# mLSTM denominators: GpSimd adds three heads' weighted scores over the source blocks, TensorE sums each direction over the partitions once

## The chip, the core and the metric

The kernel runs on one core of a Trainium2 chip. The metric is the device time of one execution in microseconds (us). The engines are named as in the profile: PE is TensorE's matmul, PEld its weight load, DVE is VectorE, ACT is ScalarE, POOL is GpSimd, SP issues the DMAs. SBUF is the working memory of 128 partitions; PSUM holds the results of matmuls.

## The reference, cut to what matters

Two layers of a transformer block on 256 latent and 256 context tokens of width 1024. Each layer has an mLSTM branch of four heads of width 128, two attentions, a merge and a feed-forward part. The first layer computes latent and context tokens, the second latent tokens only. For one head, one direction and one chunk of tokens the mLSTM is

```python
s = jnp.einsum('bhtd,bhsd->bhts', qc, kc) * w          # scores times decay weights
num = a[..., None] * jnp.einsum('bhtd,bhde->bhte', qc, C) + jnp.einsum('bhts,bhse->bhte', s, vc)
den = a * jnp.einsum('bhtd,bhd->bht', qc, n) + jnp.sum(s, axis=-1)
hc = num / jnp.maximum(jnp.abs(den), jnp.exp(-m_t))[..., None]
```

Both directions (forward and reversed) are computed and added. What the change concerns is `den`: for every head, direction and target token, the sum of the weighted scores over all source tokens.

## The kernel before, in words

The kernel doesn't scan chunk by chunk. It takes all 512 tokens (columns 0 to 255 latent, 256 to 511 context) as four source blocks `sb` of 128 tokens, 0 and 1 latent, 2 and 3 context. For a head `h` and a direction `d` it forms a tile per source block: the 128 source tokens on the partitions, the targets as columns. In the first layer the number of target columns `n` is 512, in the second 256. The columns that a block can reach differ (`lo` to `hi` in `mlstm_weights`): in the first layer 512, 512, 256 and 128 columns forwards, 512, 384, 256 and 128 backwards.

The stages of a head are these.

- `mlstm_weights` (L572): `rep` (L566) spreads a row of running maxima over the partitions by a matmul into a PSUM tile of the tag `tr`; ACT takes the exponential into a tile of tag `q` (forwards) or `wk` (backwards) at L586; POOL zeroes the future by an affine select (L592 forwards, L596 backwards), on all four blocks in the first layer and on blocks 0 and 1 in the second.
- `mlstm_scores` (L601) takes the source blocks in two halves, (2, 3) and then (0, 1). Per block one PE matmul of keys and queries goes into a PSUM tile of tag `s`, of which there are two; DVE multiplies it into the weights of both directions, in place (L608). The `s` tiles of the second half can be written only when DVE has read those of the first.
- `mlstm_values` (L611): per weighted tile a PE matmul with the values adds to the numerator, in `acc` forwards and in `tr` backwards. Then, for the same tiles, a PE matmul with a stationary operand of 32 columns of `cst` sums the tile over its partitions into the tile `den` (tag `mm`). Which of the four groups of 32 PSUM partitions it writes depends on the block's parity and the direction: `c = 32 * (2 * (sb % 2) + d)`. Row `4 * d + h` within the group is the head's; the other 31 rows get zeros.
- `mlstm_heads` (L627) runs the scores one half ahead of the values, head after head; `other(g)` adds the query projections of the windowed attention behind heads 2 and 3.
- `mlstm_den` (L649) copies `den`, adds the four groups by one matmul and takes the reciprocal.

All matmuls are issued at L135 and are known by their tiles: `tr<-pt,sel` is `rep`, `s<-m,m` a score, `acc<-q,y` and `tr<-wk,y` the numerators, `mm<-q,cst` and `mm<-wk,cst` the denominators, `mm<-hx,whi` and `mm<-hx,wlo` a projection. An f32 matmul shows as two instructions in the trace.

The order of the instructions on each engine is set when the program is built, by a scheduler that takes what it holds ready; an engine works strictly in that order. All DMAs go through SP. Weight blocks arrive in `wraw` and are split by ACT (L192) and DVE (L193) into a high and a low part, some blocks ahead of their use.

Of the kernel before, what the change touches and what calls it, by code (L numbers as in the profile page):

```python
# [11 lines left out]
F32R = mybir.dt.float32r  # L12
AF = mybir.ActivationFunctionType
ALU = mybir.AluOpType
# [6 lines left out]
RS_K = 0.5 * RS_C  # L21
# [16 lines left out]

# feature blocks of the input projection, in the order in which they are packed
B_Q, B_K, B_V, B_O = 0, 4, 8, 12  # L40
# [3 lines left out]
NW_IN = 52  # L44
# the gates have a bias row only: their weights come apart
B_IF = NW_IN
NB_IN = NW_IN + 1

# columns of the packed shape constants
C_ID, C_ONE, C_BD, C_MOD, C_COS, C_SIN = 0, 128, 129, 131, 133, 389  # L50
C_MA, C_MB, C_SUM, C_STRIP, C_IFS = 645, 773, 901, 965, 1028
NCST = 1156

# columns of the packed small parameters
P_BIN = 0
# [24 lines left out]
class Blank:  # L80
    """Stands for the chip while the order of the weight blocks is collected."""

# [10 lines left out]
class Net:  # L93
    def __init__(self, nc, tc, es, io, out, plan=None):
# [7 lines left out]
            "hx": pool("hx", 16), "m": pool("m", 9), "y": pool("y", 16), "wk": pool("wk", 5), "pt": pool("pt", 4),  # L102
            "q": pool("q", 12), "n": pool("n", 3), "g": pool("g", 2), "h": pool("h", 6),
            "sm": pool("sm", 12), "sn": pool("sn", 6), "sc": pool("sc", 8),
# [36 lines left out]

# [1 line left out]
    def split_weights(self, hi, lo, raw, src):  # L143
# [3 lines left out]
    def weights(self, name, idx, kb=8, width=128):  # L147
        """High and low parts of a block in pieces of width columns, fetched in the order in which they are used."""
        key = (name, idx, kb, width)
        self.used.append(key)  # L150
        if self.plan is None:
            return [(self.nc, self.nc)] * (kb * 128 // width)
        while self.sent < min(len(self.plan), len(self.used) + self.ahead):
            k = self.plan[self.sent]
            self.ready[k] = self.fetch(*k)
            self.sent += 1
        return self.ready.pop(key)
# [30 lines left out]

# [1 line left out]
    def split(self, hi, lo, x):  # L190
# [4 lines left out]
    def rms_columns(self, parts, n, inv, cols, nc_):  # L195
        """1 / sqrt(mean + EPS) of every token, up to the factor RS_K that the gains carry, tokens on the partitions.

        parts: squares, features on the partitions; cols: [128, nc_] picks the features of each group."""
        nc = self.nc
# [21 lines left out]
    def inv_rms(self, parts, n, inv, cols, nc_, tag):  # L221
        """The same on all the partitions, tokens along the free axis."""
        nt = n // 128
# [8 lines left out]

# [1 line left out]
    def setup(self):  # L234
# [54 lines left out]
    def mod_dve(self, blk):  # L289
        """One block of the modulation: features on the partitions, sums along the free axis."""  # L290
        nc = self.nc
# [47 lines left out]

# [1 line left out]
    def sumsq(self, parts, j, c0, c1, on_dve=False):  # L341
# [33 lines left out]

# [1 line left out]
    def bias(self, l, blk):  # L377
# [22 lines left out]
    def proj_v(self, l, hx):  # L400
        """Values of all the heads of the mLSTM, tokens on the partitions."""
        pss = [self.big(t) for t in ("mm", "s", "mm", "s")]
# [14 lines left out]
    def proj_values(self, l, hx):  # L417
        """Values of both attentions, tokens on the partitions: by two blocks of tokens, then by attention."""
        pss = [self.big("mm") for _ in range(2)]
# [75 lines left out]

# [1 line left out]
    def gate_weights(self, l):  # L497
# [4 lines left out]
    def gate_part(self, ps, w, k, x):  # L502
        """One feature block of the 16 gate columns; four blocks side by side on the array."""
        r = 32 * (k % 4)
        self.mm(ps[r:r + 32], w[:, 32 * k:32 * k + 32], x, k < 4, k >= 4)
# [54 lines left out]
    def stack_rows(self, rows, n):  # L560
        """Rows as F32R high parts on partitions 0-63 and low parts on 64-127."""
        o = self.big("pt", F32R)
# [9 lines left out]
    def mlstm_weights(self, h, n, rows):  # L572
        """Decay weights by (direction, source block): the tile and the columns that hold them."""
        nc = self.nc
# [36 lines left out]
    def mlstm_values(self, h, n, half, v, wt, num, den):  # L611
        parts = []
        for d in range(2):
            for i, sb in enumerate(MSB[half][::1 - 2 * d]):
# [4 lines left out]
                for a, b in pieces:  # L619
                    self.mm(num[d][:, a:b], v[sb][:, 128 * h:128 * h + 128], w[:, a:b], i + half == 0, i + half == 2)  # L620
                    parts.append((d, sb, w, a, b))
        for d, sb, w, a, b in parts:
            r, c = 4 * d + h, 32 * (2 * (sb % 2) + d)
            self.mm(den[c:c + 32, a:b], self.cst[:, C_STRIP + 31 - r:C_STRIP + 63 - r], w[:, a:b],
                    False, h == NH - 1 and half == 1)

    def mlstm_heads(self, n, q, k, v, rows, den, other):  # L627
        """Numerators of all the heads; the scores run one half of the source blocks ahead of the values."""
        nums, prev = [], None
        for h in range(NH + 1):  # L630
            for half in range(2):
                if h < NH:
                    if half == 0:
                        wt = self.mlstm_weights(h, n, rows)
                    self.mlstm_scores(n, half, q[h], k[h], wt)
                if prev is not None:
                    g, ghalf, gwt = prev
                    if ghalf == 0:
                        num = [self.big("acc"), self.big("tr")]
                    self.mlstm_values(g, n, ghalf, v, gwt, num, den)  # L640
                    if ghalf == 1:
# [20 lines left out]
    def mlstm_sum(self, h, n, nums, r, sums):  # L662
        """Both directions of a head together, and the sums of its squares as rows: high and low parts of a
        row lie 16 partitions apart."""
        nc = self.nc
# [36 lines left out]

# [1 line left out]
    def scores(self, l, pair, q, k, ctx, window, qb):  # L704
# [59 lines left out]
    def attention(self, l, heads, n, ys, fill):  # L764
        """heads: (pair, q, k, v, window) by name of the result; one unit of scores runs ahead of the values."""
        nc = self.nc
# [30 lines left out]

# [1 line left out]
    def gate(self, l, i, j, hx, n):  # L799
# [16 lines left out]

# [1 line left out]
    def residual(self, l, which, j, ps, c0, c1):  # L818
# [45 lines left out]
    def scaled_hx(self, hx, l, j):  # L864
        """The block before the norm's factor, and the shift as the columns after it."""
        nc = self.nc
# [55 lines left out]

# [1 line left out]
    def layer(self, l, hx, n, first, gates):  # L924
# [322 lines left out]
def build(arrays):  # L1247
    nc = bacc.Bacc("TRN2", target_bir_lowering=False, num_devices=1)
    io = {k: nc.dram_tensor(k, a.shape, F32, kind="ExternalInput").ap() for k, a in arrays.items()}
# [14 lines left out]
```

## Time and profile before

| what | value |
|---|---|
| median of 3 runs | 1526.93 us (1526.5 to 1527.32) |
| profiled execution, span | 1523.1 us |
| PE busy | 1507.0 us, 99% |
| DVE busy | 1067.4 us, 70% |
| ACT busy | 748.9 us, 49% |
| POOL busy | 31.1 us, 2% |
| chain that ended last | PE 98% |

The span is the profiled execution's time from its first instruction to its last. The trace has no wall time of its own for that execution; the median of the runs is 3.8 us above the span, and this is taken as what lies around it. The denominators stand in two short stretches: about 136 to 178 us (first layer) and 1048 to 1078 us (second layer).

### The profile page before, as it was taken

What the parts mean: (1) busy time and instruction counts of PE and PEld (TensorE: products, weight loads), DVE (VectorE), ACT (ScalarE), POOL (GpSimd) and SP (SyncE); (2) the same over time, 40 slices, a digit from 0 to 9 for tenths busy, and PEclk for the clock granted to TensorE, in tenths of its full rate; (3) what the DMA queues carried; (4) which work ended last, traced back from release to release, by engine and by line L of the source; (5) the groups of instructions that cost most, each with busy time, mean ns of one, the idle gap of its engine ahead of it and who ended that gap; (6) DMA issues with size and microseconds to landing.
All of it is one profiled execution on the core that took longest, in us unless ns stands there. A gap on an engine that the chain in (4) does not pass through costs nothing.

```text
span 1523.1 us, 25242 instructions
## 1 busy us (share of the span) xinstructions
PE 1507.0 (99%) x8999; PEld 1241.7 (82%) x9000; DVE 1067.4 (70%) x2664; ACT 748.9 (49%) x1525; POOL 31.1 (2%) x72
## 2 busy tenths in 40 slices
PE   8999999999999999999999999999999999999997
PEld 4586677777777889888888888887788889999997
DVE  5396397666558846889588677654788766776765
ACT  4444455555574334532233233653556665665553
POOL 0001100000000000000000000000100000000000
PEclk9999999999999999999999999999999999999999
DMA  9472012112125632466455553341133335566662
GB/s 333 164 237 76 24 50 91 56 62 63 63 83 180 187 97 78 151 215 209 151 193 185 189 173 118 95 131 57 59 112 111 98 105 160 168 192 182 182 179 91
DMA packets 112591, 203.74 MB, mean 134 GB/s; under 512 B 12496, under 2 KB 16336, under 8 KB 112464
## 3 DMA queue, kind: packets, MB, share of 16 engines
q1 hardware_dynamic: 112464, 202.11, 42.0%
q8 instruction: 71, 1.16, 0.3%
q14 instruction: 56, 0.46, 0.1%
HBM read 201.02 MB, written 1.05 MB: 133 GB/s over the span
## 4 chain that ended last, share of the span: by engine, by line
PE 98%; DVE 1%; ACT 0%; issue 0%; DMA 0%; ACTq 0%; DVEq 0%
PE mm L135 65%; PE s L135 21%; PE acc L135 5%; PE tr L135 4%; PE tr L748 3%; DMA h<-w_if 0%; DVE h L1059 0%; ACT m L372 0%; DVE wlo L193 0%; ACT hx L192 0%; ACT whi L192 0%; DVE y L669 0%; DVE q L485 0%; ACT h L274 0%; PE tr L555 0%
## 5 line engine op out<-in xcount | busy, mean ns | idle before, releaser
L192 ACT ACTIVATE whi<-wraw 128x512 fp32r<-128x512 f32 (+1 forms) x558 | 345.7, 625 | 515.3 <-PE mm L135 352.9
L135 PE MATMUL mm<-hx,whi 128*128 128x512 f32 (+2 forms) x2128 | 548.6, 344 | 1.9 <-ACT hx L192 1.6
L193 DVE TENSOR_TENSOR wlo<-wraw,whi 128x512 fp32r<-128x512 f32 (+1 forms) x558 | 374.4, 681 | 171.8 <-ACT whi L192 159.8
L135 PEld LDWEIGHTS mm<-hx,whi 128*128 128x128 f32 x2128 | 364.6, 189 | 60.8 <-issue 15.0
L135 PE MATMUL mm<-hx,wlo 128*128 128x512 f32 (+2 forms) x1064 | 362.3, 341 | 0.1
L135 PE MATMUL mm<-y,whi 128*128 128x256 f32 (+1 forms) x1024 | 259.7, 332 | 0.0
L135 PEld LDWEIGHTS mm<-hx,wlo 128*128 128x128 f32 x1064 | 201.1, 189 | 26.5 <-issue 4.4
L135 PE MATMUL s<-hx,whi 128*128 128x512 f32 (+2 forms) x800 | 193.5, 331 | 0.0
L135 PEld LDWEIGHTS mm<-y,whi 128*128 128x128 f32 x1024 | 176.6, 190 | 18.5 <-issue 1.5
L135 PE MATMUL mm<-y,wlo 128*128 128x256 f32 (+1 forms) x576 | 188.6, 328 | 0.0
L135 PEld LDWEIGHTS s<-hx,whi 128*128 128x128 f32 x800 | 135.6, 189 | 16.2 <-issue 2.9
L135 PE MATMUL s<-hx,wlo 128*128 128x512 f32 (+2 forms) x400 | 132.6, 332 | 0.5 <-DVE wlo L193 0.5
L135 PEld LDWEIGHTS mm<-y,wlo 128*128 128x128 f32 x576 | 109.5, 190 | 10.0 <-issue 0.5
L298 DVE SCALAR_TENSOR_TENSOR q<-q,q 128x512 f32<-128x512 f32 x160 | 105.4, 689 | 0.1
L298 DVE SCALAR_TENSOR_TENSOR h<-q,q 128x512 bf16<-128x512 f32 x160 | 104.7, 688 | 0.1
L135 PE MATMUL mm<-m,whi 128*128 128x256 f32 (+1 forms) x320 | 85.2, 320 | 0.0
L135 PEld LDWEIGHTS s<-hx,wlo 128*128 128x128 f32 x400 | 75.6, 189 | 10.2 <-issue 2.5
L135 PE MATMUL s<-q,q 128*128 128x512 f32 (+1 forms) x192 | 80.0, 424 | 0.0
L750 ACT ACTIVATE pt<-tr 128x512 f32<-128x512 f32 (+1 forms) x96 | 46.7, 525 | 29.6 <-PE tr L748 29.0
L135 PEld LDWEIGHTS mm<-m,whi 128*128 128x128 f32 x320 | 56.9, 190 | 4.4
L823 DVE SCALAR_TENSOR_TENSOR X<-mm,m,X 128x256 f32<-128x256 f32 x88 | 40.2, 482 | 24.8 <-PE mm L135 24.6
L135 PEld LDWEIGHTS s<-q,q 128*128 128x128 f32 x192 | 36.1, 188 | 24.8 <-issue 21.0
(233 smaller groups left out, 1771.8 us busy)
## 6 DMA issues: line engine op xcount, KB each, us to landing
wraw<-w_ff SPq DMA_DIRECT2D x256, 256.0 KB, 3.0
wraw<-w_in SPq DMA_DIRECT2D x206, 256.0 KB, 2.7
q<-w_mod SPq DMA_DIRECT2D x160, 256.0 KB, 3.0
wraw<-w_br SPq DMA_DIRECT2D x48, 256.0 KB, 2.7
y<-w_mod SPq DMA_DIRECT2D x32, 256.0 KB, 5.4
wraw<-w_o SPq DMA_DIRECT2D x32, 256.0 KB, 2.7
X<-x SPq DMA_DIRECT2D x4, 512.0 KB, 5.3
q<-cc SPq DMA_DIRECT2D x8, 256.0 KB, 4.7
```

What stands on the lines that cost most here:

```text
L135: self.nc.tensor.matmul(out, a, b, start=start, stop=stop)
L192: nc.scalar.activation(out=hi, in_=x, func=AF.Copy)
L193: return nc.vector.tensor_tensor(out=lo, in0=x, in1=hi.bitcast(F32), op=ALU.subtract)
L298: nc.vector.scalar_tensor_tensor(out=junk if v == 0 else raw, in0=raw, scalar=1.0, in1=self.cb[v][c], op0=ALU.mult, op1=ALU.mult, accum_ou ...
L748: self.nc.tensor.transpose(pt[:, 128 * b:128 * b + 128], p[:, 128 * b:128 * b + 128], self.ident)
L750: self.nc.scalar.activation(out=pts[-1][:, :nk], in_=pt[:, :nk], func=AF.Copy)
L823: nc.vector.scalar_tensor_tensor(out=self.X[:, j, a:b], in0=ps[:, a - c0:b - c0], scalar=self.mod[l][which][:, j, v:v + 1], in1=self.X[:, ...
```

## The change

Three of the four heads no longer have a denominator matmul per tile. When both halves of such a head are scored, POOL adds the tiles of a direction over the source blocks into one tile `pv` of 1024 columns (both directions side by side), and PE sums each direction over the partitions once: six matmuls, issued together between the two halves of the last head's values. The last head keeps its matmuls. The new matmuls of head `i` use the group of 32 rows that `i % 2` and the direction give. A pool `pv` of three tiles is added, and to make room the scratch for dynamic DMAs is set to 1024 bytes. All else in the diff is comments and blank lines.

```diff
+            "q": pool("q", 12), "pv": pool("pv", 3), ...
...
                     self.mm(num[d][:, a:b], v[sb][:, 128 * h:128 * h + 128], w[:, a:b], i + half == 0, i + half == 2)
                     parts.append((d, sb, w, a, b))
+        if h < NH - 1:
+            return
         for d, sb, w, a, b in parts:
-            r, c = 4 * d + h, 32 * (2 * (sb % 2) + d)
-            self.mm(den[c:c + 32, a:b], self.cst[:, C_STRIP + 31 - r:C_STRIP + 63 - r], w[:, a:b],
-                    False, h == NH - 1 and half == 1)
+            self.mlstm_den_part(den, h, d, sb % 2, w, a, b, half == 1)
+
+    def mlstm_den_part(self, den, h, d, i, w, a, b, stop):
+        r, c = 4 * d + h, 32 * (2 * i + d)
+        self.mm(den[c:c + 32, a:b], self.cst[:, C_STRIP + 31 - r:C_STRIP + 63 - r], w[:, a:b], False, stop)
+
+    def mlstm_weight_sums(self, n, wt):
+        nc = self.nc
+        t = self.t("pv", [128, 2 * T])
+        sums = [t[:, :n], t[:, T:T + n]]
+        for d, out in enumerate(sums):
+            order = (2, 3, 0, 1) if d == 0 else (3, 2, 1, 0)
+            (w0, _, _), (w1, _, hi) = [wt[d, sb] for sb in order[:2]]
+            nc.gpsimd.tensor_tensor(out=out[:, :hi], in0=w0[:, :hi], in1=w1[:, :hi], op=ALU.add)
+            if hi < n:
+                nc.gpsimd.tensor_copy(out[:, hi:], w0[:, hi:n])
+            for sb in order[2:]:
+                w, lo, hi = wt[d, sb]
+                nc.gpsimd.tensor_tensor(out=out[:, lo:hi], in0=out[:, lo:hi], in1=w[:, lo:hi], op=ALU.add)
+        return sums
...
                     self.mlstm_scores(n, half, q[h], k[h], wt)
+                    if half == 1 and h < NH - 1:
+                        sums.append(self.mlstm_weight_sums(n, wt))
...
+                    if g == NH - 1 and ghalf == 1:
+                        for i, pair in enumerate(sums):
+                            for d, w in enumerate(pair):
+                                self.mlstm_den_part(den, i, d, i % 2, w, 0, n, False)
                     self.mlstm_values(g, n, ghalf, v, gwt, num, den)
...
-    nc = bacc.Bacc("TRN2", target_bir_lowering=False, num_devices=1)
+    nc = bacc.Bacc("TRN2", target_bir_lowering=False, num_devices=1, dynamic_dma_scratch_size=1024)
```

The scheduler also moves other work. On PE in the first layer, head 2 (counted from 0), from its second `rep` to its second-half scores, the order before is the following; `mm_1323` is `den`, `acc_1437` and `tr_1438` are head 1's numerators, `s_1497` and `s_1501` the second-half scores of head 2.

```order
L135 MATMUL tr_1463<-pt_1320,sel 128x512
L135 MATMUL acc_1437<-q_1392,y_1071 128x128
L135 MATMUL tr_1438<-wk_1403,y_1071 128x256
L135 MATMUL tr_1438<-wk_1406,y_1069 128x128
L135 MATMUL mm_1323<-q_1389,cst 32x256
L135 MATMUL mm_1323<-q_1392,cst 32x128
L135 MATMUL mm_1323<-wk_1403,cst 32x256
L135 MATMUL mm_1323<-wk_1406,cst 32x128
L135 MATMUL mm_1323<-q_1451,cst 32x512
L135 MATMUL s_1497<-m_720,m_858 128x256
L135 MATMUL s_1501<-m_720,m_858 128x256
L135 MATMUL acc_1505<-q_1451,y_1073 128x512
```

In the changed kernel the same place of PE reads as follows; `mm_1577` is the first query projection of the windowed attention, `tr_1515` the backward numerator of head 2.

```order
L135 MATMUL tr_1468<-pt_1323,sel 128x512
L135 MATMUL acc_1447<-q_1398,y_1074 128x128
L135 MATMUL tr_1448<-wk_1409,y_1074 128x256
L135 MATMUL tr_1448<-wk_1412,y_1072 128x128
L135 MATMUL mm_1577<-hx_257,wlo_1220 128x512
L135 MATMUL mm_1577<-hx_259,whi_1219 128x512
L135 MATMUL mm_1577<-hx_260,whi_1219 128x512
L135 MATMUL mm_1577<-hx_259,wlo_1220 128x512
L135 MATMUL s_1498<-m_723,m_861 128x256
L135 MATMUL tr_1515<-wk_1470,y_1078 128x512
L135 MATMUL s_1502<-m_723,m_861 128x256
L135 MATMUL acc_1514<-q_1456,y_1076 128x512
```

Five denominator matmuls are gone from here; four matmuls of the projection, which stood behind head 2 before, have come forward, and a numerator matmul stands between the two scores. One projection matmul comes forward in head 0 and four in each of heads 1 and 2; in the second layer four more come forward in head 0.

On POOL in the first layer the affine selects of head 2 stand before like this (`q_` forwards, `wk_` backwards).

```order
L592 AFFINE_SELECT q_1451<-q_1451 128x128
L592 AFFINE_SELECT q_1454<-q_1454 128x256
L592 AFFINE_SELECT q_1457<-q_1457 128x128
L592 AFFINE_SELECT q_1460<-q_1460 128x128
L596 AFFINE_SELECT wk_1465<-wk_1465 128x128
L596 AFFINE_SELECT wk_1468<-wk_1468 128x128
L596 AFFINE_SELECT wk_1471<-wk_1471 128x128
L596 AFFINE_SELECT wk_1474<-wk_1474 128x128
```

In the changed kernel, from the same head's third forward select on, `pv_1506` being the sums of head 2:

```order
L592 AFFINE_SELECT q_1462<-q_1462 128x128
L592 AFFINE_SELECT q_1465<-q_1465 128x128
L640 TENSOR_TENSOR pv_1506<-q_1456,q_1459 128x512
L596 AFFINE_SELECT wk_1470<-wk_1470 128x128
L596 AFFINE_SELECT wk_1473<-wk_1473 128x128
L596 AFFINE_SELECT wk_1476<-wk_1476 128x128
L642 COPY pv_1506<-wk_1470 128x128
L596 AFFINE_SELECT wk_1479<-wk_1479 128x128
L640 TENSOR_TENSOR pv_1506<-wk_1470,wk_1473 128x384
L645 TENSOR_TENSOR pv_1506<-pv_1506,q_1462 128x256
L645 TENSOR_TENSOR pv_1506<-pv_1506,q_1465 128x128
L645 TENSOR_TENSOR pv_1506<-pv_1506,wk_1476 128x256
```

The add of 512 columns, which reads tiles that DVE has already multiplied, now stands in front of the backward selects of the same head; a last add of 128 columns follows, and then the selects of head 3. The order of SP, of ACT and of DVE is unchanged but for one weight split in the second layer (L192, L193), which comes forward from head 3 to the end of head 0.

## Rows read from the trace of the kernel before

**Rows 1.** The page: busy time of each engine, and the chain that ended last.
```profile
PE 1507.0 (99%) x8999; PEld 1241.7 (82%) x9000; DVE 1067.4 (70%) x2664; ACT 748.9 (49%) x1525; POOL 31.1 (2%) x72
...
PE 98%; DVE 1%; ACT 0%; issue 0%; DMA 0%; ACTq 0%; DVEq 0%
```

**Rows 2.** Windows of a head period, each layer: length, PE, PEld, DVE, ACT, POOL busy.
```profile
147.00:157.25 10.25, 10.25 (x48) 5.51 (x47) 3.69 (x9) 4.74 (x10) 2.39 (x10) 1.00 0.00 0
...
1055.30:1062.10 6.80, 6.76 (x44) 4.84 (x43) 2.77 (x9) 3.67 (x11) 1.14 (x4) 1.00 0.00 0
```

**Rows 3.** Timeline, PE, first layer: start us, duration, operation.
```profile
154.72 0.49 PE L135 MATMUL tr<-pt,sel 128*128 128x512 f32 x1
155.05 1.88 PE L135 MATMUL s<-m,m 128*128 128x512 f32 x4
156.77 0.59 PE L135 MATMUL acc<-q,y 128*128 128x256 f32 x2
...
158.49 0.40 PE L135 MATMUL mm<-q,cst 128*32 128x256 f32 x2
...
158.95 1.02 PE L135 MATMUL mm<-q,cst 128*32 128x512 f32 x2
159.90 1.13 PE L135 MATMUL s<-m,m 128*128 128x256 f32 x4
160.87 1.67 PE L135 MATMUL acc<-q,y 128*128 128x512 f32 x6
162.38 1.67 PE L135 MATMUL tr<-wk,y 128*128 128x512 f32 x4
163.98 0.40 PE L135 MATMUL mm<-q,cst 128*32 128x256 f32 x1
...
164.97 0.49 PE L135 MATMUL tr<-pt,sel 128*128 128x512 f32 x1
```

**Rows 4.** Timeline, DVE, first layer, head 2.
```profile
156.33 1.40 DVE L608 SCALAR_TENSOR_TENSOR q<-s,q 128x512 f32<-128x512 f32 x2 [4.79 <-POOL q L592]
158.81 1.16 DVE L608 SCALAR_TENSOR_TENSOR wk<-s,wk 128x512 f32<-128x512 f32 x2 [1.08 <-POOL wk L596]
```

**Rows 5.** Timeline, POOL: first-layer head 2, then two additions of 256 columns.
```profile
158.48 0.29 POOL L596 TENSOR_SCALAR_AFFINE_SELECT wk<-wk 128x128 f32<-128x128 f32 x1 [0.98 <-ACT wk L586]
...
176.69 0.64 POOL L443 TENSOR_TENSOR n<-n,cst 128x256 f32<-128x256 f32 x1 [6.49 <-DVE h L442]
...
196.62 1.14 POOL L443 TENSOR_TENSOR n<-n,cst 128x256 f32<-128x256 f32 x1 [6.47 <-DVE h L442]
```

**Rows 6.** Groups by form, POOL: busy us, mean ns of one.
```profile
L443 POOL TENSOR_TENSOR n<-n,cst 128x256 f32<-128x256 f32 x20 | 16.9, 845 | 289.6 <-DVE h L442 268.2 <-DVE sm L736 16.3 <-ACT y L671 5.1
...
L592 POOL TENSOR_SCALAR_AFFINE_SELECT q<-q 128x128 f32<-128x128 f32 x20 | 5.6, 296 | 856.9 <-ACT q L586 856.9
L592 POOL TENSOR_SCALAR_AFFINE_SELECT q<-q 128x256 f32<-128x256 f32 x4 | 1.6, 406 | 1.1 <-ACT q L586 1.1
```

**Rows 7.** Timeline, DVE, beside the first of those additions.
```profile
176.51 0.41 DVE L608 SCALAR_TENSOR_TENSOR q<-s,q 128x256 f32<-128x256 f32 x1
176.84 0.78 DVE L444 TENSOR_TENSOR h<-h,cst 128x256 f32<-128x256 f32 x1
```

**Rows 8.** Timeline, PE, second layer: parts of head 0's, then of head 2's period.
```profile
1050.62 0.62 PE L135 MATMUL mm<-q,cst 128*32 128x256 f32 x2
1051.17 1.13 PE L135 MATMUL s<-m,m 128*128 128x256 f32 x4
...
1063.38 0.40 PE L135 MATMUL mm<-q,cst 128*32 128x256 f32 x2
...
1063.94 0.70 PE L135 MATMUL acc<-q,y 128*128 128x256 f32 x2
...
1066.73 0.41 PE L135 MATMUL mm<-q,cst 128*32 128x256 f32 x2
...
1067.30 0.39 PE L135 MATMUL tr<-pt,sel 128*128 128x256 f32 x1
```

More of the change, by code (lines that the diff above doesn't have):

```diff
@@ L102, in __init__ @@
             "hx": pool("hx", 16), "m": pool("m", 9), "y": pool("y", 16), "wk": pool("wk", 5), "pt": pool("pt", 4),
-            "q": pool("q", 12), "n": pool("n", 3), "g": pool("g", 2), "h": pool("h", 6),
+            "q": pool("q", 12), "pv": pool("pv", 3), "n": pool("n", 3), "g": pool("g", 2), "h": pool("h", 6),
             "sm": pool("sm", 12), "sn": pool("sn", 6), "sc": pool("sc", 8),
@@ L621, in mlstm_values @@
                     parts.append((d, sb, w, a, b))
+        if h < NH - 1:
+            return
         for d, sb, w, a, b in parts:
-            r, c = 4 * d + h, 32 * (2 * (sb % 2) + d)
-            self.mm(den[c:c + 32, a:b], self.cst[:, C_STRIP + 31 - r:C_STRIP + 63 - r], w[:, a:b],
-                    False, h == NH - 1 and half == 1)
+            self.mlstm_den_part(den, h, d, sb % 2, w, a, b, half == 1)
[16 more added lines that the diff above has]
+        return sums
     def mlstm_heads(self, n, q, k, v, rows, den, other):
         nums, prev = [], None
+        sums = []
         for h in range(NH + 1):
```

## The prediction

> **What bounds the kernel now.** I read the page first: PE is busy for 99% of the span and is 98% of the chain that ended last [rows 1]. Then the stretches of the change, by window: in a head's period of 10.25 us in the first layer PE is busy for all of it, DVE for 3.69, ACT for 4.74 and POOL for 2.39; in the second layer the period is about 6.8, with 2.77, 3.67 and 1.14 [rows 2]. The PE timeline confirms that this is work and not waiting dressed up as work: four score passes of 512 columns start 155.05 and the next operation 156.77, so a pass takes 0.43 us, and the other operations of the period keep to that rate [rows 3]. So a matmul that leaves these stretches gives its time back, as long as what feeds PE keeps up. What feeds it is a short chain that repeats per head: rep on PE, exponential on ACT, select on POOL, multiplication on DVE, and back to PE, where the second-half scores need the two score tiles free again. POOL is in that chain, nearly empty, and the change fills it.
>
> **What is removed.** From start to start, the denominators of a head in the first layer hold PE from 158.49 to 158.95, from 158.95 to 159.90 and from 163.98 to 164.97: 0.46 + 0.95 + 0.99 = 2.40 us [rows 3]. Three heads: 7.2 us. In the second layer 1063.38 to 1063.94 and 1066.73 to 1067.30: 0.56 + 0.57 = 1.13 us [rows 8]; three heads 3.4. The first head's stand in three places there instead of two, and the additional one costs 1051.17 - 1050.62 = 0.55 [rows 8]: 3.9 us. Together 11.1 us.
>
> Beside them goes some time around them. Four score passes of 256 columns that follow a denominator take 0.97 (159.90 to 160.87), though twice the columns take 1.72; the backward numerators before one take 1.60 (162.38 to 163.98), where 896 columns in two passes at 0.43 per 512 make 1.50 [rows 3]. That is 0.1 on either side of a denominator block. I take back 0.2 per head in the first layer and 0.1 in the second, 0.9 in all; its bounds are 0 and 2 us. The Trainium skill (TensorEngine Tiling (Array Packing), Key Properties) says that changing the tiling mode drains TensorE, which fits these tenths; by it every block removed would give both sides back, near the upper bound, and the sum below would be 1.1 us better.
>
> **What is added on PE.** Six sums, each over 512 columns in the first layer and 256 in the second. A 512-column one alone takes 0.95 [rows 3]. They don't run one after the other: the block at 163.98 has 1280 columns in three row groups, over 2.1 us at 0.43 per pass and 512, and is over in 0.99 [rows 3]. The six lie in four groups, then two groups again: two rounds, 2 x 0.95 = 1.9 us, and 2 x 0.56 = 1.1 us in the second layer [rows 8]; together 3.0. From above, were nothing side by side: 6 x 0.95 + 6 x 0.48 = 8.6 us; from below, if they flow into the last head's own block without a seam, 2.5. I take 3.0, since four matmuls in four groups is what that block of the second layer is. Their inputs are long there: the last is POOL's sum of head 2, and PE has a projection and half a head to do first.
>
> **What is added on POOL.** Per head in the first layer additions of 512, 384, 256, 256, 128 and 128 columns and a copy of 128; in the second 256 four times and 128 twice. The trace has additions of 256 columns only: 0.64 at the least, 1.14 at the most, 0.845 on average [rows 5, 6]. The long ones have a reason: DVE operations with both inputs in SBUF ran beside them. The short one at 176.69 ran beside a multiplication of L608, which reads one input from PSUM, and that one kept its 0.41, while the two-SBUF-input L444 right behind it took 0.78 [rows 5, 7]. In the stretches of the change DVE does almost only L608. So I take 0.64 per 256 columns. For 512 it lies between 0.64 (all fixed cost) and 2.28 (twice the longest); a select goes from 296 to 406 ns from 128 to 256 columns [rows 6], so about 0.19 is fixed, and 0.64 + 0.45 to 2 x 0.64 gives 1.1 to 1.28: I take 1.2. A head's additions then make about 4.3 us in the first layer and 3.4 in the second; with the selects POOL has 6.7 of some 9 us, and 4.5 of some 5.5. It is not the bound.
>
> **The new wait.** In POOL's queue the 512-column addition stands before the backward selects. It waits for DVE's second multiplication, which ends 156.33 + 1.40 = 157.73, 3.0 us behind the rep at 154.72 [rows 3, 4]. The first backward select started at 158.48 (3.76 behind the rep) because only then was its exponential there [rows 5]. With the addition in front it starts at 3.05 + 1.2 = 4.25, ends 4.55, and the backward multiplication that frees the first score tile ends at about 5.25. PE wants that tile at 158.49 - 154.72 = 3.77 plus the four projection matmuls put there, each 0.23 (half of two passes), 0.91: 4.68. So heads 1 and 2 wait 0.57 us each. In head 0 only one projection matmul covers, and the select of the second backward block is the one behind the addition: a wait of about 0.85 by the same steps. Sum 2.0 us. Each tenth on the 512-column addition costs three tenths; at 0.64 the waits are 0.3 in all, at 2.28 they are 5.2. Queued behind the waiting addition are the selects, so DVE's backward multiplications, so PE's scores: that is the chain just counted. The next head's selects stand behind the last addition, which ends about 9.0 us behind the rep, as the next rep starts (9.1) and before its first exponential is there (its multiplication starts 1.6 behind the rep [rows 3, 4], the select 0.3 earlier); no wait. In the second layer no first-half tile needs a select, so no addition stands before what PE wants next; by the same steps the last additions of a head end some 1.5 us into the next, whose selects are wanted only by its second half. No wait.
>
> The projection matmuls that come forward cost nothing: they are taken from the run behind head 2. The wk tiles that ACT overwrites for the next head are now also read by POOL, but the addition that frees the first ends a third of a period before. The DMA scratch touches no queue that SP uses, and SP's order is the same.
>
> **Sum.** -11.1 - 0.9 + 3.0 + 2.0 = -7.0 us. The trace's span is 1523.1; it becomes 1516.1, and with the 3.8 us between span and median, 1519.9. PE is the chain before and behind both stretches [rows 1], so the rest of the kernel only starts earlier.
>
> **Rivals.**
> 1. GpSimd is the bound: its additions take 1.14 per 256 columns throughout. A head has then 7.4 + 0.3 + 2.4 = 10.1 us of POOL in the first layer and 5.7 + 1.15 = 6.85 in the second, just the periods of now. The first layer keeps 1.1 us in each of two heads (four projection matmuls are done inside) and 1.0 around them, the second 1.6, less 3.0: -1 to -2, about 1525.5. For it: the mean of the rows is 0.845. Against it: their cause is absent here. The Trainium skill (GPSIMD Engine Reference, Engine selection) advises against two-input elementwise work on GpSimd, about twice as slow as VectorE. Its measured 4497 ns for 2048 columns would make an estimate of 1.1 us for 512; by that the waits are 0.3 us less and the forecast stands.
> 2. Slower: POOL's additions and DVE's L608 shut each other out, whatever L608 reads, so that multiplications, additions and selects of a head stand in one line. With additions of 0.64 the line is 3.69 + 4.3 + 2.4 = 10.4 us, under the 10.25 + 0.91 at which the first layer begins to lose, and the second layer's 2.77 + 3.4 + 1.15 = 7.3 is over its 6.8: three times -0.8, twice +0.5 and 3.0 for the six sums, 1528.5. With additions stretched to 1.14 the lines are 13.8 and 9.6: three times 2.6, twice 2.8 and 3.0 make 16.4, 1543. Between them 1535. Against it: rows 7, where L608 was not held.
> 3. The adds are hidden but the gain is not passed on, because the freed score tile comes only with the second backward multiplication (0.55 us later in three heads) and the six sums run singly (up to 8.6): -7.0 + 1.6 + 5.6, about 1527. For it: nothing in the trace; against it the two places in which groups overlap.
>
> **Chances.** Forecast 0.76, rival 1 0.12, rival 2 0.05, rival 3 0.07. Less than 0.2% (3 us) either way is no change that can be told. The forecast's own bounds: -9.8 (short additions, 1.1 more around the blocks) to -3.7 (the 512-column addition at 2.28). All of it counts as faster: 0.78 with a little of rival 1; no change 0.16; slower 0.06. The range takes in the forecast and half of rival 1.
>
> **What would show it.** Right: a first-layer head period of about 9.1 us with four projection matmuls inside, second-layer periods of about 5.5, the denominator sums within 2 us behind the last head's first half, POOL's 512-column additions at 1.1 to 1.3 us and L608 with unchanged durations. Wrong: idle time of PE in front of `s<-m,m` of over 1 us ended by DVE, POOL without gaps, L608 of 512 columns above 0.7 us, or PE waiting for `pv`.

## The result and the profile after

The changed kernel takes 1518.81 us (median of 4 executions, 1517.88 to 1519.34), the kernel before in the same comparison 1527.12 us (4 executions, 1526.50 to 1528.26). The ratio is 0.9945, with a 95% interval of 0.9933 to 0.9958: faster, since the whole interval lies below 1. 1519.9 was predicted, with a range of 1517 to 1525; the gain is 8.3 us, where 7.0 were forecast.

The page after, its span and the lines that answer to [rows 1]:

```profile
span 1516.2 us, 25137 instructions
...
PE 1498.8 (99%) x8922; PEld 1240.0 (82%) x8922; DVE 1067.3 (70%) x2664; ACT 747.1 (49%) x1525; POOL 56.1 (4%) x111
...
PE 96%; DVE 1%; ACT 1%; POOL 1%; issue 0%; ACTq 0%; POOLq 0%; DVEq 0%
```

POOL works 25 us more and PE 8.2 us less; PE is still nearly the whole chain, but POOL has come into it.

The best measure of the change is a stretch that begins and ends on PE at the same work in every kernel: from head 0's first rep (`tr<-pt,sel`) to the first projection matmul behind the last head's denominators. Both kernels have 24 projection matmuls inside it, in either layer. Windows of it, first layer and then second: length, busy time of PE, PEld, DVE, ACT, POOL; first of the kernel before, then of the changed one.

```profile
135.50:181.91 46.41, 46.41 (x210) 26.29 (x209) 19.37 (x41) 22.08 (x46) 10.16 (x33) 1.00 0.06 18
1047.43:1078.10 30.67, 30.56 (x194) 22.32 (x192) 15.80 (x43) 17.02 (x45) 5.48 (x17) 1.00 0.07 23
```
```profile
137.59:179.82 42.23, 40.25 (x169) 24.76 (x167) 19.54 (x41) 21.68 (x46) 23.92 (x54) 1.00 0.06 19
1045.15:1071.37 26.22, 26.17 (x159) 21.64 (x157) 15.80 (x43) 16.74 (x45) 16.67 (x35) 1.00 0.09 33
```

The first layer is 4.18 us shorter and the second 4.45: 8.63 us. In the first, PE now idles for 42.23 - 40.25 = 1.98 us, where before it never did. DVE's busy time has hardly moved, POOL's has more than doubled. Outside the two stretches little differs: between them lie 865.52 us before and 865.33 after, behind the second 445.0 and 444.8; only the start is 2.09 us longer in the changed kernel's execution (first rep at 137.59 instead of 135.50), of which more below. The head periods, answering to [rows 2]:

```profile
145.12:154.50 9.38, 8.65 (x34) 5.44 (x33) 3.68 (x8) 4.65 (x10) 8.10 (x18) 1.00 0.00 0
154.50:163.79 9.29, 8.66 (x34) 5.44 (x33) 3.78 (x8) 4.65 (x10) 7.02 (x16) 1.00 0.01 3
1055.56:1060.86 5.30, 5.30 (x29) 4.47 (x27) 2.99 (x10) 3.59 (x10) 4.79 (x11) 1.00 0.01 3
```

Where PE idles is told by its timeline in head 2 of the first layer, which answers to [rows 3]. The first line of the list of PE's waits (us in total, times, longest) is new, `s` waiting for DVE's multiplication:

```profile
PE s L135 <- DVE wk L608: 2.0, 3, 0.7
```

The timeline (start us, duration, operation, in brackets the idle time before it):

```profile
154.50 0.69 PE L135 MATMUL tr<-pt,sel 128*128 128x512 f32 x1
...
157.72 0.82 PE L135 MATMUL tr<-wk,y 128*128 128x256 f32 x4
158.30 0.47 PE L135 MATMUL mm<-hx,wlo 128*128 128x512 f32 x1
158.61 0.63 PE L135 MATMUL mm<-hx,whi 128*128 128x512 f32 x2
159.07 0.40 PE L135 MATMUL mm<-hx,wlo 128*128 128x512 f32 x1
160.10 0.70 PE L135 MATMUL s<-m,m 128*128 128x256 f32 x2 [0.63 <-DVE wk L608]
```

And POOL and DVE there, answering to [rows 4, 5]:

```profile
157.79 1.29 POOL L640 TENSOR_TENSOR pv<-q,q 128x512 f32<-128x512 f32 x1 [0.31 <-DVE q L608]
159.03 0.78 POOL L596 TENSOR_SCALAR_AFFINE_SELECT wk<-wk 128x128 f32<-128x128 f32 x3
...
159.36 1.15 DVE L608 SCALAR_TENSOR_TENSOR wk<-s,wk 128x512 f32<-128x512 f32 x2 [1.65 <-POOL wk L596]
```

The 512-column addition waits for DVE's pair of multiplications, holds POOL until 159.08, the backward select comes behind it, DVE multiplies at 159.36 (4.86 us behind the rep, before it was 158.81 - 154.72 = 4.09), and PE, through with its four projection matmuls, stands idle for 0.63 us.

Additions by shape, one group for each width (busy us, mean ns of one), answering to [rows 6]:

```profile
L640 POOL TENSOR_TENSOR pv<-q,q 128x512 f32<-128x512 f32 x3 | 3.8, 1282 | 0.7 <-DVE q L608 0.7
L640 POOL TENSOR_TENSOR pv<-wk,wk 128x384 f32<-128x384 f32 x3 | 3.0, 998 | 0.0
L645 POOL TENSOR_TENSOR pv<-pv,wk 128x256 f32<-128x256 f32 x6 | 4.4, 726 | 0.0
L645 POOL TENSOR_TENSOR pv<-pv,wk 128x128 f32<-128x128 f32 x6 | 2.7, 455 | 0.5
```

The six sums, in the first layer and in the second, each with the operation behind it (start us, duration):

```profile
175.74 2.08 PE L135 MATMUL mm<-pv,cst 128*32 128x512 f32 x12
177.75 0.92 PE L135 MATMUL acc<-q,y 128*128 128x256 f32 x4
...
1068.32 1.05 PE L135 MATMUL mm<-pv,cst 128*32 128x256 f32 x12
1069.30 0.92 PE L135 MATMUL acc<-q,y 128*128 128x256 f32 x4
```

They take 2.01 and 0.98 us.

### The profile page after: what moved, and what is told of

Its sections match the earlier page's. It is cut to its first block, busy times and chain, and to the rows that moved or that the text cites. A ratio compares the mean times of both kernels' runs of the same rounds, so it can differ in the third digit from the quotient of the medians.

```text
span 1516.2 us, 25137 instructions
## 1 busy us (share of the span) xinstructions
PE 1498.8 (99%) x8922; PEld 1240.0 (82%) x8922; DVE 1067.3 (70%) x2664; ACT 747.1 (49%) x1525; POOL 56.1 (4%) x111
## 4 chain that ended last, share of the span: by engine, by line
PE 96%; DVE 1%; ACT 1%; POOL 1%; issue 0%; ACTq 0%; POOLq 0%; DVEq 0%
PE mm L135 64%; PE s L135 21%; PE acc L135 5%; PE tr L135 4%; PE tr L776 3%; ACT h L372 0%; DVE h L1087 0%; ACT q L586 0%; POOL pv L640 0%; ACT hx L192 0%; DVE wlo L193 0%; POOL pv L645 0%; DVE q L608 0%; ACT whi L192 0%; POOL wk L596 0%
## 5 line engine op out<-in xcount | busy, mean ns | idle before, releaser
L192 ACT ACTIVATE whi<-wraw 128x512 fp32r<-128x512 f32 (+1 forms) x558 | 344.9, 624 | 512.6 <-PE mm L135 356.0
L193 DVE TENSOR_TENSOR wlo<-wraw,whi 128x512 fp32r<-128x512 f32 (+1 forms) x558 | 373.9, 680 | 169.0 <-ACT whi L192 157.3
```

Source lines behind the costliest of these rows:

```text
L192: nc.scalar.activation(out=hi, in_=x, func=AF.Copy)
L193: return nc.vector.tensor_tensor(out=lo, in0=x, in1=hi.bitcast(F32), op=ALU.subtract)
```

## Experiments

My theory after the result: the gain is PE's time of the denominators, with the seams around them, less the six sums, less three waits that POOL's 512-column addition makes by its place in POOL's queue. The rivals: part of the gain lies outside the span and comes from the smaller scratch; POOL is the bound; POOL and DVE hold each other up. The table has the stretches defined above, from one profiled execution each, and the medians (against 1527.1 to 1527.8 us of the kernel before).

| kernel | first layer, us | second layer, us | median, us | ratio to before, 95% |
|---|---|---|---|---|
| before | 46.41 | 30.67 | | |
| before, small scratch | 46.46 | 30.67 | 1527.57 | 1.0001 (0.9991 to 1.0011) |
| changed | 42.23 | 26.22 | 1518.81 | 0.9945 (0.9933 to 0.9958) |
| second layer alone | 46.42 | 26.23 | 1520.70 | 0.9961 (0.9948 to 0.9973) |
| without POOL's additions | 40.13 | 26.23 | 1516.29 | 0.9925 (0.9912 to 0.9939) |
| without PE's six sums | 40.55 | 25.36 | 1516.06 | 0.9922 (0.9907 to 0.9937) |
| additions behind two selects | 40.22 | 26.23 | 1516.61 | 0.9931 (0.9918 to 0.9945) |
| additions on DVE | 40.16 | 26.22 | 1516.39 | 0.9919 (0.9900 to 0.9938) |
| an addition twice, second layer | 42.24 | 27.43 | 1520.13 | 0.9950 (0.9935 to 0.9965) |
| behind two selects, and sums split | 39.82 | 26.01 | 1516.28 | 0.9920 (0.9906 to 0.9934) |

**The scratch alone.**

```diff
-    nc = bacc.Bacc("TRN2", target_bir_lowering=False, num_devices=1)
+    nc = bacc.Bacc("TRN2", target_bir_lowering=False, num_devices=1, dynamic_dma_scratch_size=1024)
```

> The kernel before with one number changed, the reservation for descriptors of dynamic DMAs (1024 bytes, as the changed kernel has it, in place of the default). Theory A (part of the measured gain lies outside the span): the span stays within 0.5 us of that of the kernel before, and the time outside the span falls from about 3.7 us to about 1.7 us, so that the whole time falls by about 2.0 us, to about 1525 us. Rival B (the reservation is only memory, and the time outside the span follows from the work): span and time outside the span both as before, difference 0 within 0.5 us.

Measured: no difference (ratio 1.0001), and theory A is gone: in each of its 11 executions, and in each of the 15 of the kernel before beside them, the time outside the span is 1.7 to 1.8 us. Most of what I had taken for time outside the span was the start of the program. The 15 spans of the kernel before go from 1523.2 us, at a mean granted clock of 0.998, to 1529.6 us, at 0.991. In the ten profiles kept, the granted clock is 1.00 from 30 to 1500 us in every one; it differs between them in the first 30 us, ahead of the stretches of the change. One window of three profiles there, PE's granted clock third from the end: the kernel before, the changed kernel, and the one with its additions on DVE.

```profile
24.00:28.00 4.00, 3.80 (x23) 1.65 (x23) 3.63 (x7) 1.58 (x5) 0.00 (x0) 1.00 0.73 218
```
```profile
24.00:28.00 4.00, 4.00 (x17) 1.92 (x19) 3.86 (x8) 2.20 (x4) 0.00 (x0) 0.57 0.81 291
```
```profile
24.00:28.00 4.00, 3.52 (x17) 2.04 (x18) 3.08 (x8) 3.14 (x6) 0.00 (x0) 0.70 0.69 225
```

A granted clock of 1.00 is the level of 2.4 GHz; 0.57 is a stretch that lay mostly at 1.2 GHz. Ahead of it, in the changed kernel, PE had idled for 1.58 us at about 21 us, waiting for ACT; it did so in the kernel before as well, where the clock stayed at 1.00, so that the idle time alone does not decide it. Head 0's first rep then comes at 135.50, 137.59 and 139.07 us in these three. So the profiled execution of before was one with a good start (1523.1 us and 1.7, below every one of the four executions in the comparison), and that of the changed kernel was not; spans of two single executions differ by 6.9 us here, though the stretches differ by 8.63 and the medians by 8.3. Good starts come in the changed kernels too: at the same mean clock of 0.998 the kernel before has a span of 1523.2 us and the kernel with its additions behind two selects one of 1512.6, 10.6 us less, which is what their stretches differ by (77.08 and 66.45).

**The second layer alone.**

```diff
-        if h < NH - 1:
+        if h < NH - 1 and n == SEQ:
             return
...
-                    if half == 1 and h < NH - 1:
+                    if half == 1 and h < NH - 1 and n == SEQ:
```

> The change in the second layer alone (with the changed kernel's reservation for descriptors); the first layer sums its denominators on TensorE as before. From the two profiles the stretch from the second layer's first rep to the projection behind its heads went from 30.67 to 26.22 us and the first layer's from 46.41 to 42.23 us. Theory A (each layer's gain is its own and passed on to the end): span 4.4 us shorter than before's, and the time outside it as that of the other run with this reservation, thus 1520.5 to 1522.7 us, the rest (about 4.2 us less the start-up's luck) coming with the first layer. Rival B (the gain of the second layer is not passed on, the tail of the layer waits for something else): within 1 us of the kernel before.

Measured: the first layer stays at 46.42 us and the second is at 26.23, 4.44 below before. Its profiled execution has the same kind of start as the one of the kernel with the small scratch (first reps at 135.65 and 135.76), so the two spans can be compared: 1518.9 and 1523.4, 4.5 us. The gain of the second layer is passed on whole, and theory A holds.

**The waits: POOL's order, and no additions.** In the first kernel the additions of a first-layer head stand behind the head's second backward select (`sel`; `self.after` tells the scheduler to issue them behind it); in the second they are gone, and the six sums read constants. The order of PE's work in the stretches is that of the changed kernel in both.

```diff
+                        if sb == 2:
+                            self.sel2nd = sel
...
+                        with (self.after(self.sel2nd) if n == T else nullcontext()):
                             sums.append(self.mlstm_weight_sums(n, wt))
```

> The changed kernel, with GpSimd's sums of a head in the first layer put behind the second backward select of the head instead of ahead of both; TensorE's order stays the same. Theory A (the 512-column addition of 1.28 us ahead of the backward selects is what makes the s tiles late, 0.62 + 0.72 + 0.63 us): the three waits of TensorE on the multiplication from wk vanish, span 2.0 us shorter than the changed kernel's, about 1516.9 us. Rival B (GpSimd is full and the work that is moved back makes the next head's selects late instead): the waits come back one half later, no gain, 1518 to 1520 us. Rival C (something other than the select holds that multiplication): waits stay at about 0.7 us each.

```diff
-                        sums.append(self.mlstm_weight_sums(n, wt))
+                        sums.append([self.cst[:, :n]] * 2)
```

> The changed kernel without GpSimd's additions: TensorE's six sums read constants in their place, so the denominators of three heads lack their sums. Theory A (the additions cost only the three waits in the first layer, 2.0 us): 2.0 us less than the changed kernel, about 1516.8 us, and the waits for the multiplication from wk gone. Rival B (GpSimd's and VectorE's accesses shut each other out): VectorE's multiplications from L608 get shorter too (from 0.69 to 0.6 us or less for 512 columns) and 4 us or more come back, in the second layer too. Rival C (the additions are free): no difference within 0.5 us.

Measured: 40.22 and 40.13 us in the first layer, 2.01 and 2.10 below the changed kernel, and the wait on `wk` is off both lists. POOL in head 2 with the order changed:

```profile
157.20 0.30 POOL L596 TENSOR_SCALAR_AFFINE_SELECT wk<-wk 128x128 f32<-128x128 f32 x1 [1.04 <-ACT wk L586]
157.67 0.30 POOL L596 TENSOR_SCALAR_AFFINE_SELECT wk<-wk 128x128 f32<-128x128 f32 x1 [0.17 <-ACT wk L586]
157.93 1.27 POOL L642 TENSOR_TENSOR pv<-q,q 128x512 f32<-128x512 f32 x1
159.16 0.53 POOL L596 TENSOR_SCALAR_AFFINE_SELECT wk<-wk 128x128 f32<-128x128 f32 x2
```

The same addition costs nothing where the two selects that PE waits for go first: two selects moved ahead of one instruction give all that leaving the additions out gives, but for 0.1 us. So POOL is not full in the first layer (B), nothing else holds the multiplication (C), and what else the additions cost there is within that 0.1 us. That they don't lengthen DVE's multiplications either is shown by these, with the additions (the changed kernel) and without:

```profile
L608 DVE SCALAR_TENSOR_TENSOR q<-s,q 128x512 f32<-128x512 f32 x8 | 5.4, 690 | 9.7 <-POOL q L592 9.7
```
```profile
L608 DVE SCALAR_TENSOR_TENSOR q<-s,q 128x512 f32<-128x512 f32 x8 | 5.5, 692 | 9.4 <-POOL q L592 9.4
```

**No sums.**

```diff
-                        for i, pair in enumerate(sums):
-                            for d, w in enumerate(pair):
-                                self.mlstm_den_part(den, i, d, i % 2, w, 0, n, False)
+                        pass
```

> The changed kernel without TensorE's six sums in either layer (GpSimd still adds; the denominators of three heads are left out). Theory A (six sums cost what their rows span, 2.01 us from 175.74 to 177.75 in the first layer and 0.98 us in the second): the stretch from the first rep of head 0 to the projection behind the heads is 2.0 us shorter in the first layer (42.23 to 40.2 us) and 1.0 us in the second (26.22 to 25.2 us), the whole 3.0 us below the changed kernel, about 1515.8 us. Rival B (the sums fill a time in which TensorE would wait anyway, for the last head's products): under 1.5 us in all, a wait appears in their place.

Measured: 1.68 us less in the first layer and 0.86 in the second, 2.54 together; no wait came in their place (PE's waits on `wk` are 2.0 us, as in the changed kernel). The expectation of 3.0 was 0.46 too much, because the rows of the sums begin while the block ahead of them still runs. Without them, the last head's denominators in the first layer and what follows:

```profile
176.00 0.27 PE L135 MATMUL mm<-q,cst 128*32 128x128 f32 x1
176.43 0.92 PE L135 MATMUL acc<-q,y 128*128 128x256 f32 x4
```

From the last denominator matmul to the numerators it is 0.43 us here; in the changed kernel the sums start 0.11 behind it. So 0.32 us of the sums' row lie in time that the block ahead takes without them too: 2.01 - 0.32 = 1.69. In the second layer the same two steps are 0.32 and 0.20 us, and 0.98 - 0.12 = 0.86.

**Additions on DVE.** Each `nc.gpsimd` of the additions becomes `nc.vector`.

```diff
-            nc.gpsimd.tensor_tensor(out=out[:, :hi], in0=w0[:, :hi], in1=w1[:, :hi], op=ALU.add)
+            nc.vector.tensor_tensor(out=out[:, :hi], in0=w0[:, :hi], in1=w1[:, :hi], op=ALU.add)
```

> The changed kernel with the additions (and the one copy) on VectorE in place of GpSimd, TensorE's order unchanged. A full-width VectorE addition of 512 columns is taken at 0.68 us (its weight subtraction), against GpSimd's 1.28. Theory A (the loss is only the addition ahead of the backward weights): in head 0 the wait goes; in heads 1 and 2 the addition now stands on VectorE ahead of the backward multiplications and the wait shrinks from 0.7 to about 0.1 us; first layer 1.8 us shorter. In the second layer VectorE's busy time rises from 2.99 to about 4.9 of 5.30 us per head, still under TensorE's: no change; in all about 1517 us. Rival B (VectorE becomes the bound in the second layer, since its additions stand in order among multiplications that TensorE needs): the second layer's head period grows above 5.5 us and the whole is 1518 us or more.

Measured: 40.16 and 26.22 us, and the waits are gone. DVE's timeline in head 2 of the first layer, and a window of a second-layer head (DVE's busy time third behind the length):

```profile
157.69 0.69 DVE L640 TENSOR_TENSOR pv<-q,q 128x512 f32<-128x512 f32 x1
158.74 1.16 DVE L608 SCALAR_TENSOR_TENSOR wk<-s,wk 128x512 f32<-128x512 f32 x2 [0.35 <-POOL wk L596]
```
```profile
1055.24:1060.54 5.30, 5.26 (x29) 4.56 (x27) 4.71 (x15) 3.59 (x10) 1.27 (x4) 1.00 0.01 2
```

The addition stands ahead of the backward multiplications here too, but it is 0.69 us long instead of 1.28 and DVE had the time: it still waits 0.35 us for the select behind it. At 4.71 of 5.30 us in the second layer DVE holds nobody up (B falls). So what decides is whether the addition delays the backward multiplication: on POOL it delays that one's select, on DVE it is done before the select is.

**How much room POOL has in the second layer.**

```diff
-            nc.gpsimd.tensor_tensor(out=out[:, :hi], in0=w0[:, :hi], in1=w1[:, :hi], op=ALU.add)
+            for _ in range(2 if d == 0 and n == SEQ else 1):
+                nc.gpsimd.tensor_tensor(out=out[:, :hi], in0=w0[:, :hi], in1=w1[:, :hi], op=ALU.add)
```

> The changed kernel with GpSimd's first forward addition of each of three heads in the second layer (256 columns, 0.73 us) done twice. TensorE's order unchanged. In the changed kernel's second layer GpSimd has gaps of 0 to 0.3 us per head, and 1.06 us in the last. Theory A (GpSimd is nearly full there, but its results are wanted 1 to 2 us after they come, so that the slack lies in TensorE's order): of the 3 x 0.73 = 2.2 us, 0 to 0.7 us reach the end. Rival B (GpSimd is the bound of the second layer already): all 2.2 us come through, about 1521 us.

Measured: 27.43 us, 1.21 of the 2.2 us come through: between A and B, and A's bound of 0.7 was too low. PE's waits in its timeline, then two of POOL's additions for head 0 and its first forward selects of heads 1 and 2:

```profile
1051.56 1.23 PE L135 MATMUL s<-m,m 128*128 128x256 f32 x4 [0.15 <-DVE wk L608]
1057.62 1.23 PE L135 MATMUL s<-m,m 128*128 128x256 f32 x4 [0.70 <-DVE wk L608]
1063.14 1.23 PE L135 MATMUL s<-m,m 128*128 128x256 f32 x4 [0.16 <-DVE wk L608]
```
```profile
1051.13 1.81 POOL L646 TENSOR_TENSOR pv<-pv,q 128x256 f32<-128x256 f32 x2
...
1054.12 0.30 POOL L592 TENSOR_SCALAR_AFFINE_SELECT q<-q 128x128 f32<-128x128 f32 x1
...
1059.65 0.29 POOL L592 TENSOR_SCALAR_AFFINE_SELECT q<-q 128x128 f32<-128x128 f32 x1
```

POOL now runs without a gap, and a head takes it 1059.65 - 1054.12 = 5.53 us, 0.23 more than PE's period of 5.30 in the changed kernel. PE's periods of heads 1 and 2 are 5.52 and 6.07 us, and the last head's part of the stretch is 10.73 instead of 10.51: 0.22, 0.77 and 0.22 more. The 0.55 by which the middle one stands out is the length of one addition: the last backward selects of heads 0, 1 and 2, which those three scores wait for, start at 1050.87, 1056.95 and 1062.47, 6.08 and 5.52 us apart, and between the first two stands the row of 1.81 us, whose two additions take 1.26 in the other heads. The one of 128 columns in it took 1.00 us instead of 0.46. The changed kernel has the same long addition (0.97 us), beside a weight split on DVE that reads two inputs from SBUF:

```profile
1050.00 1.78 POOL L645 TENSOR_TENSOR pv<-pv,q 128x256 f32<-128x256 f32 x2
...
1050.78 0.68 DVE L193 TENSOR_TENSOR wlo<-wraw,whi 128x512 fp32r<-128x512 f32 x1
```

There it delays nothing that PE waits for. Without the doubled addition a head needs 5.53 - 0.73 = 4.80 us of POOL, so the changed kernel's second layer is half a microsecond per head from having POOL as its bound.

**A better version.** POOL's order as above, and the third head's two sums on PE cut into column halves, so that they use four groups of rows instead of two.

```diff
-                                self.mlstm_den_part(den, i, d, i % 2, w, 0, n, False)
+                                if i < 2:
+                                    self.mlstm_den_part(den, i, d, i, w, 0, n, False)
+                        for d, w in enumerate(sums[2]):
+                            self.mlstm_den_part(den, 2, d, 0, w, 0, n // 2, False)
+                        for d, w in enumerate(sums[2]):
+                            self.mlstm_den_part(den, 2, d, 1, w, n // 2, n, False)
```

> The kernel with GpSimd's sums behind the second backward select in the first layer, and the third head's two sums on TensorE cut into two column halves each, so that four of them stand on four column groups of the array instead of two on two. Theory A (matmuls on four different column groups run beside each other, so six sums take two rounds and a round of half the columns takes half the time): the sums' stretch falls from 2.0 to 1.5 us in the first layer and from 1.0 to 0.75 in the second, 0.75 us below the kernel with the sums moved alone, about 1515.9 us. Rival B (sums do not overlap by group, the time goes by the columns streamed in all): no change, 1516.6 us.

```profile
173.94 1.68 PE L135 MATMUL mm<-pv,cst 128*32 128x512 f32 x16
175.54 0.92 PE L135 MATMUL acc<-q,y 128*128 128x256 f32 x4
...
1066.12 0.83 PE L135 MATMUL mm<-pv,cst 128*32 128x256 f32 x16
1066.88 0.92 PE L135 MATMUL acc<-q,y 128*128 128x256 f32 x4
```

The sums take 1.60 and 0.76 us instead of 2.01 and 0.98, in place of the expected 1.5 and 0.75; the stretches are 0.40 and 0.22 shorter. Theory A holds: groups overlap. The medians, 1516.28 against 1516.61 us without the split, agree but could not show it alone. It is the shortest version by its stretches, 11.25 us (46.41 + 30.67 - 39.82 - 26.01) under the kernel before.

## Why the prediction was right, step by step

The time fell into the range because the mechanism was the one forecast; two sizes were off, both to the good side. The terms, from the stretches (the first two are what is left when the others are taken out):

| term | predicted, us | measured, us | from |
|---|---|---|---|
| denominators and seams, first layer | -7.8 | -7.8 | -4.18 - 2.0 (idle) - 1.68 (sums) |
| denominators and seams, second layer | -4.2 | -5.3 | -4.45 - 0.86 (sums) |
| six sums | +3.0 | +2.5 | 1.68 + 0.86 |
| waits | +2.0 | +2.0 to 2.1 | the two kernels without them |
| sum | -7.0 | -8.6 | |

- **Waits.** Forecast 0.57, 0.57 and 0.85 us for heads 1, 2 and 0. Against the kernel without additions the periods of heads 1 and 2 are 9.38 - 8.72 = 0.66 and 9.29 - 8.71 = 0.58 us longer, and that of head 0 7.53 - 6.65 = 0.88. By PE's idle time in the timeline the three are 0.72, 0.63 and 0.62. The 512-column addition took 1.28 where 1.2 was taken, and the chain behind it was as described. This is the step on which most hung, and the two kernels that remove the wait in different ways show it.
- **Additions.** 0.73 us per 256 columns, not 0.64; why the shortest one before was shorter is open. POOL's load came out above the forecast: 7.0 and 8.1 us in the two windows of a first-layer period instead of 6.7, and 4.79 instead of 4.5 in the second layer. "It is not the bound" held, but in the second layer with 0.5 us per head to spare.
- **Seams.** This is the term that was mis-sized. A second-layer head's period fell by 6.82 - 5.30 = 1.52 us from rep to rep, of which its denominators' rows explain 0.56 + 0.57 = 1.13 [rows 8]; 0.39 is seam. The backward numerators and what follows them, in the kernel before (a denominator block and rep follow, at 1066.73 and 1067.30 [rows 8]) and in the changed one (rep follows at once):

```profile
1065.77 1.03 PE L135 MATMUL tr<-wk,y 128*128 128x256 f32 x4
...
1067.52 1.03 PE L135 MATMUL s<-m,m 128*128 128x256 f32 x4
```
```profile
1054.02 1.03 PE L135 MATMUL s<-m,m 128*128 128x256 f32 x4
1054.88 1.03 PE L135 MATMUL tr<-wk,y 128*128 128x256 f32 x4
1055.56 0.47 PE L135 MATMUL tr<-pt,sel 128*128 128x256 f32 x1
1055.86 1.12 PE L135 MATMUL s<-m,m 128*128 128x256 f32 x4
```

From the numerators to the scores it is 1.75 us before and 0.98 after: 0.77 less, for a block whose row is 0.57, so that its two seams are 0.20. Ahead of a block four passes of 256 columns take 0.96 us, ahead of other full-size work 0.86 (1054.02 to 1054.88). So a seam is about 0.1 us on either side, as the prediction read it from the first layer; what it had wrong is the count. It took 0.1 per head in the second layer, where a head has two blocks with two sides each. Seven blocks went from that layer, with 3.94 us in rows and 5.31 in all: 1.37, or 0.20 per block. In the first layer the rows of seven blocks are 7.33 us, and 7.84 - 7.33 = 0.5 us is left for their seams, as forecast (0.6) but less per block; PE's order changed there too, and no run takes this apart. The Trainium skill (TensorEngine Tiling (Array Packing), Key Properties) says that a change of tiling mode drains TensorE; the trace agrees in that time is lost at each such change, and the 1.1 us that the prediction would have gained by that rule is what the second layer brought beyond the forecast.
- **Sums.** As rows they took 2.0 and 1.0 us, as forecast (1.9 and 1.1). Their price is 2.5, because they begin while the last head's block still runs: that is the lower bound which the prediction gave for sums that flow into this block without a seam.
- **The base.** Adding 3.8 us to the span "between span and median" was right as arithmetic and wrong as a picture: 1.7 us lies outside the span, the rest was the good start of the one execution that was profiled.
- **Rivals.** POOL as the bound (1): not in the first layer, near it in the second, where POOL has two gaps, 0.17 and 0.32 us, from the first head's first select to the last head's; "POOL without gaps", a sign of being wrong, was almost met. POOL and DVE shutting each other out (2): L608 takes 690 and 692 ns with and without the additions beside it; it reads one input from PSUM. The Trainium skill (SBUF — State Buffer, Who interferes with whom) says that a DVE instruction with at most one input in SBUF, outside the two-port performance modes, does not contend with GpSimd, and the trace agrees. The one long addition stands beside a DVE instruction that reads both inputs from SBUF, as the longest one before the change did (196.62 [rows 5]). The gain not passed on (3): each layer's gain reached the end, and the sums run side by side.

## What to carry to other kernels

Work that moves to an idle engine costs what it delays in that engine's queue: here three instructions of 1.28 us cost 2.0 us by standing ahead of selects that PE needed, and 0.1 us or less two instructions later. Compare kernels on a stretch that starts and ends at the same instruction, since spans of single executions of one kernel differed by up to 6 us. When small matmuls of another tile shape leave a stream of full ones, count the change of shape on both sides of each block, in the stage where it happens.

## What the runs showed of the hardware

- GpSimd's float32 additions with both inputs in SBUF take 455, 726, 998 and 1282 ns for 128, 256, 384 and 512 columns: about 0.18 us and 2.15 ns per column (from the first and the last). VectorE's take 689 ns for 512 and 419 for 256, so GpSimd is 1.9 and 1.7 times as slow.
- A GpSimd addition of 128 columns took 0.97 us in the changed kernel (1.00 in the one with an addition done twice) where VectorE's weight split, with both inputs in SBUF, ran beside it, and 0.46 elsewhere. VectorE's 256-column additions beside GpSimd's selects took up to 0.52 us instead of 0.42.
- A block of matmuls with 32 stationary columns between full-size ones cost 0.20 us more than its own row in the second layer, 0.1 on either side; in the first, where PE's order changed too, 0.07 per block were left.
- Six sums in four groups and two groups take 2.01 us, in four and four (the last half as long) 1.60: matmuls on different groups of 32 rows overlap, and leaving two groups empty costs.
- Spans of one and the same kernel went from 1523.2 us at a mean granted clock of 0.998 to 1529.6 at 0.991. In the profiles kept, the clock ahead of 1500 us differs in the first 30 us alone. What decides it was not tried.
